# A decoder layer on one NeuronCore: the up-projection's seven products chained in one PSUM bank and interleaved across neighbouring gates, GpSimd's sums moved to VectorE, the down-projection's loads in a fixed order

## The chip, the cores and the metric

The kernel runs on one core of one Trainium2 chip. The metric is the device time of one execution in microseconds (us), lower is better. The time of a kernel is the median of its runs.

## What is computed

One hybrid decoder layer on 1024 tokens of width 1024, all in float32: two groups of token mixers (causal "forgetting" attention and a gated linear recurrence), one output projection, a residual with LayerNorm, a gated MLP with a causal convolution of width 3, and a last residual with LayerNorm. The change touches what follows the mixers:

```python
    mix = jnp.concatenate([o_a, o_r], axis=-1).astype(dtype) @ w_o[l]
    x = _layer_norm(DEEPNORM_ALPHA * x + mix, ln_mix_g[l], ln_mix_b[l])

    h = _causal_depthwise_conv(x @ w_up[l], conv_w[l], conv_b[l])
    a, u = jnp.split(h, 2, axis=-1)
    ffn = (jax.nn.gelu(a, approximate=False) * u) @ w_down[l]
    x = _layer_norm(DEEPNORM_ALPHA * x + ffn, ln_ffn_g[l], ln_ffn_b[l])
```

The width of the MLP is 2816, which is 22 tiles of 128 columns.

## The kernel before

Every float32 matrix product is made of three matmuls in a reduced format: both operands are split into a high and a low part (ScalarE rounds the high part, VectorE subtracts it to get the low part), and high·high, high·low and low·high are added up in PSUM. Tiles with a name ending in h and l, or the two halves of a tile `w` or `dw`, are such parts. A scheduler orders the instructions on each engine when the kernel is built; an engine executes its own list strictly in that order. `tc.issue_after` pins an instruction behind another one on the same engine. In the code `tt` and `stt` are VectorE's tensor_tensor and scalar_tensor_tensor, `gt_` is GpSimd's tensor_tensor, `act` and `nc.scalar.copy` are ScalarE, `mm` is TensorE.

**Output projection and first LayerNorm (L1156 to L1205).** The tokens stand in eight tiles of 128 rows. Tiles 4 to 7 are projected earlier, among the mixers; the loop at L1184 makes tiles 3, 2, 1, 0: 48 matmuls each (L1197), the residual on VectorE (L1199), LayerNorm (L267). `second_half`, `first_half` and `both_halves` then form the seven left operands that Strassen's scheme in Winograd's form needs for the MLP: "22", "s1", "11", "12", "s2", "s4", "s3". They are halves of token tiles or sums and differences of those halves. `unit` (L1145) transposes each with four TensorE transposes (L1149), and ScalarE and VectorE split the result (L1152, L1153).

**Up-projection (L1214 to L1342).** For each of 22 MLP tiles, called gates, `prep` (L1228) loads two weight tiles of 512 KB and forms four sums of weight halves on GpSimd (L1238 to L1241). `product` (L1245) splits one weight combination (L1248 on ScalarE, L1249 on VectorE) into one of eight buffers `w`, and issues 4 x 3 = 12 matmuls of 512 columns (L1254). A gate has seven products, in the order 1, 6, 2, 5, 7, 3, 4, into four PSUM banks `b[0]` to `b[3]`; odd and even gates use two sets of banks (`ps` and `pb` in the rows). Product 2 adds onto product 1 in `b[0]`, so ScalarE must first copy product 1 out (L1291, tile `s`); likewise product 3 follows a copy of product 5 (L1293). VectorE forms the other sums (L1295 to L1306); the convolution is one ScalarE activation and VectorE multiply-adds for each half of 512 tokens (L1280 to L1284); then GELU (L1310), the product of the two branches on GpSimd (L1311), every second gate four more sums on GpSimd (L1321 to L1324), and stores to `hd` in DRAM from GpSimd's queue.

**Down-projection (L1347 to L1524).** Seven products again, each of six chunks (`part`, L1426): a weight chunk `k0` or `k1` (`load_k`, L1376) and a stored chunk `ar` (`araw`, L1364) are loaded on SyncE's queue, both are split (L1372, L1373) into a ring of buffers `dw`, and up to 24 matmuls follow (L1446). Sums of weight halves are formed on GpSimd (L1433 to L1437, L1466). The residual rows `acc` are loaded back (L1452) and added. The last product (L1486) is followed tile by tile by the final LayerNorm (`finish`, L1398), whose last addition is GpSimd's (L1417).

## Time and profile before

| | |
|---|---|
| median of 3 runs | 1396.06 us (1393.99 to 1400.61) |
| the profiled execution, its own time | 1390.83 us |
| its span in the trace | 1389.0 us |
| mean granted TensorE clock | 0.975 of full speed |

The span is what the profiler's records cover; the 1.8 us between it and the execution's own time lie around it. Busy time of an engine is the time in which one of its instructions ran; a wait is the idle time just before an instruction, put down to the event that came last. TensorE's granted clock has two levels, 2.4 GHz (1.00 in the rows) and 1.2 GHz (0.50); a mean in between mixes the two. A VectorE or ScalarE instruction's record begins before the one ahead of it has ended, so the pace of a row of them is the distance of their starts and not the listed duration. PE is TensorE, DVE VectorE, ACT ScalarE, POOL GpSimd, SP SyncE.

### The profile page before, as it was taken

What the parts mean: (1) busy time and instruction counts of PE and PEld (TensorE: products, weight loads), DVE (VectorE), ACT (ScalarE), POOL (GpSimd) and SP (SyncE); (2) the same over time, 40 slices, a digit from 0 to 9 for tenths busy, and PEclk for the clock granted to TensorE, in tenths of its full rate; (3) what the DMA queues carried; (4) which work ended last, traced back from release to release, by engine and by line L of the source; (5) the groups of instructions that cost most, each with busy time, mean ns of one, the idle gap of its engine ahead of it and who ended that gap; (6) DMA issues with size and microseconds to landing.
All of it is one profiled execution on the core that took longest, in us unless ns stands there. A gap on an engine that the chain in (4) does not pass through costs nothing.

```text
span 1389.0 us, 17673 instructions
## 1 busy us (share of the span) xinstructions
PE 1298.2 (93%) x6457; PEld 1070.8 (77%) x6457; DVE 1080.2 (78%) x1517; ACT 632.4 (46%) x1045; POOL 528.9 (38%) x460
## 2 busy tenths in 40 slices
PE   6899999999999997999499999999999999899996
PEld 5888877877878886888487787778878787688886
DVE  8758686786646667668979999999999977665695
ACT  4246655654555645432353444444444443334351
POOL 4122222131332223003536556656655644850016
PEclk9999999999999999999799999999999999999998
DMA  8311211143433357423122223223223249633333
GB/s 291 137 31 31 76 31 61 41 123 127 97 101 95 83 126 207 155 84 118 76 91 92 82 92 114 99 91 114 80 76 111 99 127 390 252 97 96 99 99 114
DMA packets 68567, 156.45 MB, mean 113 GB/s; under 512 B 6720, under 2 KB 22080, under 8 KB 68480
## 3 DMA queue, kind: packets, MB, share of 16 engines
q1 hardware_dynamic: 57584, 116.78, 27.7%
q0 software_dynamic: 10896, 38.54, 7.4%
q8 instruction: 51, 0.84, 0.3%
q14 instruction: 36, 0.29, 0.1%
HBM read 99.98 MB, written 41.68 MB: 102 GB/s over the span
## 4 chain that ended last, share of the span: by engine, by line
PE 51%; DVE 25%; issue 8%; DMA 6%; ACT 6%; POOL 2%; SPq 1%; POOLq 0%; DVEq 0%; ACTq 0%
PE ps L1254 8%; PE pb L1254 7%; PE ps L235 5%; PE pb L1446 4%; PE ps L1446 4%; DVE w L1249 3%; PE pb L219 3%; PE ps L840 3%; PE pb L1197 2%; DVE yu L1282 2%; PE ps L961 2%; DMA ar<-hd 2%; DVE ya L1282 2%; PE pb L235 2%; PE pb L381 2%
## 5 line engine op out<-in xcount | busy, mean ns | idle before, releaser
L1249 DVE TENSOR_TENSOR w<-wt,w 128x512 fp32r<-128x512 f32 x88 | 128.1, 1455 | 5.8 <-ACT w L1248 5.7
L1249 DVE TENSOR_TENSOR w<-wraw,w 128x512 fp32r<-128x512 f32 x66 | 103.4, 1567 | 11.7 <-ACT w L1248 11.7
L209 POOL TENSOR_TENSOR wlo<-wraw,whi 128x1024 fp32r<-128x1024 f32 x20 | 51.9, 2593 | 135.2 <-ACT whi L208 107.5
L1446 PE MATMUL pb<-dw 128*128 128x512 f32 x396 | 94.3, 399 | 4.1 <-DVE dw L1373 4.1
L1446 PE MATMUL ps<-dw 128*128 128x512 f32 x396 | 92.9, 394 | 3.4 <-ACT dw L1372 2.0
L1446 PEld LDWEIGHTS pb<-dw 128*128 128x128 f32 x396 | 75.4, 191 | 22.6 <-DVE dw L1373 5.0
L1446 PEld LDWEIGHTS ps<-dw 128*128 128x128 f32 x396 | 74.1, 188 | 21.4 <-ACT dw L1372 2.4
L1311 POOL TENSOR_TENSOR ya<-ya,yu 128x1024 f32<-128x1024 f32 x21 | 50.8, 2420 | 101.8 <-ACT ya L1310 101.8
L1373 DVE TENSOR_TENSOR dw<-k,dw 128x1024 fp32r<-128x1024 f32 (+1 forms) x36 | 51.1, 1418 | 49.5 <-PE pb L1446 21.2
L1372 ACT CAST dw<-k 128x1024 fp32r<-128x1024 f32 (+1 forms) x36 | 35.0, 978 | 82.7 <-issue 33.5
L235 PE MATMUL ps<-xhi,whi 128*128 128x512 f32 x144 | 60.3, 419 | 1.3 <-DVE mo L739 1.3
L912 DVE TENSOR_REDUCE sml<-pb 128x1 f32<-128x896 f32 (+3 forms) x64 | 47.6, 751 | 15.7 <-PE pb L909 15.4
L1248 ACT CAST w<-wraw 128x512 fp32r<-128x512 f32 x66 | 40.6, 615 | 38.8 <-PE pb L1254 18.6
L235 PE MATMUL ps<-xlo,whi 128*128 128x512 f32 x144 | 58.0, 403 | 0.0
L219 PE MATMUL pb<-xhi,whi 128*128 128x512 f32 x176 | 57.7, 406 | 0.0
L219 PE MATMUL pb<-xhi,wlo 128*128 128x512 f32 x176 | 57.4, 400 | 0.0
L235 PE MATMUL ps<-xhi,wlo 128*128 128x512 f32 x144 | 57.4, 399 | 0.0
L1240 POOL TENSOR_TENSOR wt<-wraw,wt 128x512 f32<-128x512 f32 x22 | 29.3, 1330 | 72.3 <-DVE w L1249 72.1
L1248 ACT CAST w<-wt 128x512 fp32r<-128x512 f32 x88 | 54.3, 617 | 4.2 <-POOL wt L1238 1.7
L219 PE MATMUL pb<-xlo,whi 128*128 128x512 f32 x176 | 55.8, 398 | 0.0
L1373 DVE TENSOR_TENSOR dw<-ar,dw 128x1024 fp32r<-128x1024 f32 (+1 forms) x36 | 45.5, 1263 | 8.9 <-ACT dw L1372 8.6
L1372 ACT CAST dw<-ar 128x1024 fp32r<-128x1024 f32 (+1 forms) x36 | 35.1, 975 | 25.2 <-PE pb L1446 12.0
(439 smaller groups left out, 4082.1 us busy)
## 6 DMA issues: line engine op xcount, KB each, us to landing
wraw<-in_wup_dram SPq DMA_DIRECT2D x44, 512.0 KB, 3.6
ar<-hd SPq DMA_DIRECT2D x35, 512.0 KB, 3.6
wraw<-in_wt_dram SPq DMA_DIRECT2D x24, 512.0 KB, 3.7
hd<-sab POOLq DMA_DIRECT2D x22, 512.0 KB, 3.2
k<-in_wdn_dram SPq DMA_DIRECT2D x20, 512.0 KB, 10.1
hd<-ya POOLq DMA_DIRECT2D x11, 512.0 KB, 4.0
xres<-xin POOLq DMA_DIRECT2D x8, 512.0 KB, 4.1
wraw<-in_wo_dram SPq DMA_DIRECT2D x8, 512.0 KB, 5.3
```

The lines of the kernel that those rows point to most:

```text
L209: (nc.gpsimd.tensor_tensor if nlw[0] in PW else tt)(lo[:, ks], raw[:, ks], f(hi[:, ks]), ALU.subtract)
L219: mm(ps[:, h * 512:(h + 1) * 512], lhsT=l[:, k, :], rhs=r[:, k, h * 512:(h + 1) * 512], start=k == 0 and n == 0, stop=k == KT - 1 and n == 2)
L235: last_mm[0] = mm(ps, lhsT=l[:, k, :], rhs=r[:, k, h * 512:(h + 1) * 512], start=k == 0 and n == 0, stop=k == KT - 1 and n == 2)
L912: nc.vector.tensor_reduce(sml[:, 0:1], ps[:, 0:n], AX.X, ALU.max, negate=True)
L1248: nc.scalar.copy(sl[:, 0], w[n])
L1249: tt(sl[:, 1], w[n], f(sl[:, 0]), ALU.subtract)
L1254: last_mm[0] = mm(ps, lhsT=sl[:, wq, k], rhs=xq[:, k], start=bool(first and k == 0 and q == 0), stop=k == KH - 1 and q == 2, skip_group_ch ...
L1282: stt(y[:, o + d:o + 512], src[:, 0:512 - d], cw(t, 2 - d), y[:, o + d:o + 512], ALU.mult, ALU.add)
L1311: (tt if tail else gt_)(ya[:, hs], ya[:, hs], yu[:, hs], ALU.mult)
L1372: nc.scalar.copy(hi, raw)
L1373: tt(lo, raw, f(hi), ALU.subtract)
L1446: last_mm[0] = mm(sets[bset][t], lhsT=l[:, z, t * P:(t + 1) * P], rhs=r[:, z], start=bool(first and m + z == 0 and l is ah and r is bh), s ...
```

## The change

Five things change; the mixers before them stay as they are.

1. GpSimd's sums go to VectorE: the four weight sums of `prep`, the product after GELU, the four sums of every second gate, the sums of halves of token tiles ahead of the up-projection, and the sums of weight halves in the down-projection. GpSimd keeps its DMA queue, the reciprocal square roots and the last addition of `finish`.
2. In a gate the products 1, 6, 5, 3 are chained in one bank (`u[:, 0]`), with a ScalarE copy after 1, 6 and 5; 7 and 4 share another (`a[:, 1]`). VectorE's sums per gate fall from five to three, and the convolution runs over 1024 tokens at once. The order on TensorE is 6, 7, 5 of this gate, 1 of the next, 3 of this, 2 of the next, 4 of this.
3. The first gate is special: its weights are prepared before the output projection's loop, and its products 5 and 4, which need only the token tiles 4 to 7, run among the transposes of tiles 3, 2 and 1.
4. The LayerNorms of tiles 3, 2 and 1 become two VectorE instructions each; the statistics of tiles 2 and 1 are made on ScalarE, which writes its unused output over the projection's PSUM tile. Tile 0 is handled in column halves.
5. In the down-projection all loads are issued in program order (`fetch`), and the first residual is added after the second product's third chunk instead of before it.

```diff
-                gt_(y[:, R], y[:, L], y[:, R], ALU.add)
+                tt(y[:, R], y[:, L], y[:, R], ALU.add)
...
+            def sums(i):
 
                 y, z = xrs[i], xrs[4 + i]
                 tt(z[:, R], z[:, R], y[:, L], ALU.subtract)
-                gt_(z[:, L], y[:, L], z[:, L], ALU.subtract)
-                tt(y[:, L], y[:, R], z[:, R], ALU.subtract)
-                unit("12", y[:, R], i)
-                unit("s2", z[:, R], i)
-                unit("s4", y[:, L], i)
-                unit("s3", z[:, L], i)
+                tt(z[:, L], y[:, L], z[:, L], ALU.subtract)
+                s4s[i] = f1a.tile([P, 512], F32, name="s4", tag="u2") if i == 0 else y[:, L]
+                tt(s4s[i], y[:, R], z[:, R], ALU.subtract)
...
-                        for h in range(2):
-                            hs = slice(h * 512, (h + 1) * 512)
-                            mm(ps[:, hs], lhsT=lhs(i, j, k), rhs=r[:, k, hs],
-                               start=ki == 0 and nn == 0, stop=ki == KT - 1 and nn == 2)
-                stt(xr, xr, ALPHA, ps, ALU.mult, ALU.add)
-                layer_norm(cp, xr, xr, *gb1, add=nc.gpsimd.tensor_tensor if i in LNXP else tt, mode=LNX[i])
-                second_half(i)
-                if i < 3:
-                    first_half(i + 1)
-            first_half(0)
+                        last_mm[0] = mm(ps[:, hs], lhsT=lhs(i, j, k), rhs=r[:, k, hs],
+                                        start=k == KORD[0] and nn == 0, stop=k == KORD[-1] and nn == 2)
+                if i:
+                    stt(xr, xr, ALPHA, ps, ALU.mult, ALU.add)
+                    if i == 3:
+                        layer_norm(cp, xr, xr, *gb1, mode="S")
+                if i in (1, 2):
+                    mv = cp.tile([P, 4], F32, name="lnmv", tag="lnmv", bufs=2)
+                    act(ps, xr, AF.Copy, scale=1.0 / D, accum_out=mv[:, 0:1])
+                    act(mv[:, 3:4], mv[:, 0:1], AF.Copy, scale=-1.0)
+                    act(ps, xr, AF.Square, bias=mv[:, 3:4], accum_out=mv[:, 1:2])
+                    ts(mv[:, 1:2], mv[:, 1:2], 1.0 / D, LN_EPS, ALU.mult, ALU.add)
+                    nc.gpsimd.tensor_tensor(mv[:, 2:3], mv[:, 1:2], mhalf, ALU.pow)
+                    stt(xr, xr, mv[:, 0:1], gb1[0], ALU.subtract, ALU.mult)
+                    stt(xr, xr, mv[:, 2:3], gb1[1], ALU.mult, ALU.add)
+                if i == 0:
+                    st = cp.tile([P, 12], F32, name="lnst", tag="lnst", bufs=2)
+                    mv = cp.tile([P, 4], F32, name="lnmv", tag="lnmv", bufs=2)
+                    for h, hs in enumerate((L, R)):
+                        stt(xr[:, hs], xr[:, hs], ALPHA, ps[:, hs], ALU.mult, ALU.add)
+                        nc.vector.bn_stats(st[:, 6 * h:6 * h + 6], xr[:, hs])
+                    nc.vector.bn_aggr(mv[:, 0:2], st)
+                    ln_rstd(mv, False)
+                    for hs in (L, R):
+                        stt(xr[:, hs], xr[:, hs], mv[:, 0:1], gb1[0][:, hs], ALU.subtract, ALU.mult)
+                    for hs in (L, R):
+                        stt(xr[:, hs], xr[:, hs], mv[:, 2:3], gb1[1][:, hs], ALU.mult, ALU.add)
+                nc.gpsimd.dma_start(a1d[i], xr)
+                if i > 1:
+                    second_half(2 * i - 3)
+                    second_half(2 * i - 4)
+                if i:
+                    unit("11", xr[:, L], i)
+                    sums(i)
...
-                gt_(t12[:, 0], b12, b11, ALU.subtract)
-                gt_(t12[:, 1], b22, t12[:, 0], ALU.subtract)
-                gt_(t34[:, 1], b21, t12[:, 1], ALU.subtract)
-                gt_(t34[:, 0], b22, b12, ALU.subtract)
...
-                order = ((4, 3, 1, 1), (5, 2, 1, 0), (1, 0, 1, 0), (2, 0, 0, 1), (6, 1, 1, 0), (3, 2, 0, 1), (7, 1, 0, 1)) \
-                    if p == 0 else \
-                    ((1, 0, 1, 0), (6, 1, 1, 0), (2, 0, 0, 1), (5, 2, 1, 0), (7, 1, 0, 1), (3, 2, 0, 1), (4, 3, 1, 1))
...
+                def step(self, n):
+
+                    a, u, s1, u2, u4 = self.a, self.u, self.s1, self.u2, self.u4
                     if n == 1:
-                        nc.scalar.copy(s1, b[0])
+                        self.mul(1, u[:, 0])
+                        nc.scalar.copy(s1, u[:, 0])
+                    if n == 2:
+                        self.mul(2, a[:, 0])
+                        tt(a[:, 0], a[:, 0], s1, ALU.add)
+                    if n == 6:
+                        self.mul(6, u[:, 0], False)
+                        nc.scalar.copy(u2, u[:, 0])
+                    if n == 7:
+                        self.mul(7, a[:, 1])
                     if n == 5:
-                        nc.scalar.copy(s5, b[2])
+                        self.mul(5, u[:, 0], False)
+                        nc.scalar.copy(u4, u[:, 0])
+                    if n == 3:
+                        self.mul(3, u[:, 0], False)
+                        tt(u[:, 1], a[:, 1], u4, ALU.add)
+                        self.outs()
+                        self.conv(1)
+                    if n == 4:
+                        self.mul(4, a[:, 1], False)
+                        tt(a[:, 1], a[:, 1], u2, ALU.add)
+                        self.conv(0)
+                        self.end()
...
+                def end(self):
+                    j, (ya, yu) = self.j, self.y
+                    act(ya, ya, AF.Gelu)
+                    tt(ya, ya, yu, ALU.mult)
+                    half = NFF // 2
+                    if j < half:
+                        ys[j] = ya
+                        nc.gpsimd.dma_start(hd_[0, j], ya[:, L])
+                        return
                     m = j - half
                     ye = ys.pop(m)
-                    et_ = tt if tail else gt_
+                    tail = self.p == NFF - 1
                     sa, sb = (pl.tile([P, 2, 512], F32, name="sab", tag=tg)
                               for pl, tg in (((qkp, "ql"), (cp, "crow")) if tail else ((gv, "g0"), (gv, "g1"))))
-                    et_(sb[:, 0], ye[:, L], ye[:, R], ALU.subtract)
-                    et_(sa[:, 0], ye[:, R], ya[:, R], ALU.add)
-                    et_(sa[:, 1], sa[:, 0], ye[:, L], ALU.subtract)
-                    et_(sb[:, 1], ya[:, L], sa[:, 1], ALU.subtract)
+                    tt(sb[:, 0], ye[:, L], ye[:, R], ALU.subtract)
+                    tt(sa[:, 0], ye[:, R], ya[:, R], ALU.add)
+                    tt(sa[:, 1], sa[:, 0], ye[:, L], ALU.subtract)
+                    tt(sb[:, 1], ya[:, L], sa[:, 1], ALU.subtract)
...
+            work = chain(g.first_parts(5), g.first_parts(4))
+            for _ in range(2):
+                next(work)
+            for i in (3, 2, 1):
+                for n, src in (("12", xrs[i][:, R]), ("s2", xrs[4 + i][:, R]), ("s4", s4s[i]), ("s3", xrs[4 + i][:, L])):
+                    placed(n, src, i)
+                    next(work, None)
...
+                g, nxt = nxt, (Gate(p + 1) if p + 1 < NFF else None)
+                for n, of in ((6, g), (7, g), (5, g), (1, nxt), (3, g), (2, nxt), (4, g)):
+                    if of is not None:
+                        of.step(n)
...
+            def fetch(dst, src):
+
+                with tc.issue_after(last_ld[0].ins) if last_ld[0] is not None else ExitStack():
+                    last_ld[0] = nc.sync.dma_start(dst, src)
+
+            def bsum(dst, a, b):
+
+                with tc.issue_after(last_lo[0].ins):
+                    tt(dst, a, b, ALU.subtract)
...
-                    gt_(k0[c][:, :, L], k0[c][:, :, R], k0[c][:, :, L], ALU.subtract)
+                    bsum(k0[c][:, :, L], k0[c][:, :, R], k0[c][:, :, L])
                 if n == 6:
-                    gt_(k0[c][:, :, L], k1[c][:, :, R], k0[c][:, :, L], ALU.subtract)
+                    bsum(k0[c][:, :, L], k1[c][:, :, R], k0[c][:, :, L])
                 if n == 7:
-                    gt_(k0[c][:, :, R], k1[c][:, :, R], k0[c][:, :, R], ALU.subtract)
+                    bsum(k0[c][:, :, R], k1[c][:, :, R], k0[c][:, :, R])
...
-                        gt_(k0[c][:, :, L], k1[c][:, :, L], k0[c][:, :, L], ALU.subtract)
+                        tt(k0[c][:, :, L], k1[c][:, :, L], k0[c][:, :, L], ALU.subtract)
...
+                    if n == 5 and c == 2:
+                        residual(range(4), L)
+                        for t in range(4):
+                            stt(acc[:, t, L], acc[:, t, L], ALPHA, sets[0][t], ALU.mult, ALU.add)
```

Where the instructions stand is read from the built order of each engine. On ScalarE, around the end of a gate's last product 4: `ya` from the last bank is the convolution of the old gate, the COPY is the one that a product of the next gate waits for. Before:

```order
L1280 ACTIVATE yu_7725<-ps2_7710,ppt_76 128x512
L1248 CAST w_8032<-wraw_8018 128x512
L1280 ACTIVATE ya_7724<-ps3_7711,ppt_76 128x512
L1291 COPY s15_7879<-pb0_7865 128x512
L1248 CAST w_8048<-wt_8022 128x512
L1310 ACTIVATE ya_7724<-ya_7724 128x1024
```

and now:

```order
L1188 CAST w_7236<-wt_7082 128x512
L1316 ACTIVATE ya_7035<-ca_6808,ppt_76 128x1024
L1335 COPY u2_6955<-cu_6953 128x512
L1188 CAST w_7252<-wt_7083 128x512
L1188 CAST w_7267<-wt_7082 128x512
L1387 ACTIVATE ya_7035<-ya_7035 128x1024
```

The copy still stands right behind the old gate's convolution; it is now product 6's, which product 5 waits for, where it was product 1's, which product 2 waited for.

On GpSimd, at the end of the output projection (`wt` are weight sums, `xr` token tiles, `lnmv` the LayerNorm's small tiles). Before:

```order
L1238 TENSOR_TENSOR wt_6215<-wraw_6212,wraw_6211 128x512
L1239 TENSOR_TENSOR wt_6215<-wraw_6212,wt_6215 128x512
L1166 TENSOR_TENSOR xr_5063<-xr_5063 128x512
L1164 DMA a1d_61<-xr_5215 128x1024
L249 TENSOR_SCALAR lnmv_5881<-lnmv_5881 128x1
L250 TENSOR_TENSOR lnmv_5690<-lnmv_5690,half_80 128x1
```

and now:

```order
L1200 DMA a1d_61<-xr_5215 128x1024
L251 TENSOR_TENSOR lnmv_5690<-lnmv_5690,half_80 128x1
L251 TENSOR_TENSOR lnmv_5897<-lnmv_5897,half_80 128x1
L1255 DMA a1d_61<-xr_5836 128x1024
L1200 DMA a1d_61<-xr_5342 128x1024
```

The wide sums are gone from GpSimd there; what is left are stores and one-column roots.

On VectorE, at the change from the up-projection to the down-projection (L1348 is the last gate's sum after product 4, `dw` are the low parts of the first chunks):

```order
L1318 SCALAR_TENSOR_TENSOR yu_9382<-cu_9193,ppt_76,yu_9382 128x1022
L1348 TENSOR_TENSOR ca_9192<-ca_9192,u2_9195 128x512
L1492 TENSOR_TENSOR dw_9461<-k0_9431,dw_9460 128x1024
L1492 TENSOR_TENSOR dw_9457<-ar_9454,dw_9456 128x1024
L1318 SCALAR_TENSOR_TENSOR ya_9381<-ca_9192,ppt_76,ya_9381 128x1023
```

The first two low parts now stand behind a sum that waits for the last product of the up-projection.

## Rows read from the trace of the kernel before

**Rows 1.** The page's part 1: busy us, share of the span, instructions of each engine.

```profile
PE 1298.2 (93%) x6457; PEld 1070.8 (77%) x6457; DVE 1080.2 (78%) x1517; ACT 632.4 (46%) x1045; POOL 528.9 (38%) x460
```

**Rows 2.** Windows: stretch, its us, busy us of PE, PEld, DVE, ACT, POOL; clock; DMA.

```profile
653.40:695.50 42.10, 24.63 (x117) 19.96 (x116) 41.60 (x44) 15.01 (x24) 24.64 (x21) 0.74 0.16 63
695.50:720.90 25.40, 25.09 (x123) 20.62 (x122) 18.58 (x27) 13.11 (x24) 7.12 (x5) 0.95 0.30 89
720.90:1151.10 430.20, 416.94 (x1765) 334.74 (x1763) 403.10 (x506) 188.53 (x295) 237.47 (x181) 0.98 0.30 102
1151.10:1205.00 53.90, 46.35 (x189) 36.16 (x189) 36.66 (x32) 17.58 (x19) 40.18 (x18) 0.97 0.94 348
1205.00:1371.10 166.10, 166.10 (x736) 136.00 (x736) 118.49 (x136) 66.76 (x82) 48.24 (x34) 1.00 0.33 105
1371.10:1389.00 17.90, 6.93 (x34) 6.68 (x33) 6.50 (x14) 1.46 (x3) 5.73 (x7) 0.67 0.25 88
```

**Rows 3.** Waits, 720 to 1152 us: who waited for whom, total us, times, longest us.

```profile
PE ps L1254 <- ACT s L1291: 11.6, 7, 2.5
PE pb L1254 <- ACT s L1291: 1.5, 1, 1.5
...
ACT yu L1280 <- DVE pb L1300: 59.8, 11, 7.5
...
ACT ya L1280 <- DVE pb L1306: 14.8, 9, 1.6
```

**Rows 4.** Chain of waits, one gate of 84 matmuls: start, us, what.

```profile
1112.14 19.53 PE pb L1254 x84
```

**Rows 5.** Single lines: durations in ns, min/median/max; first and last start; forms.

```profile
L1249 DVE TENSOR_TENSOR w<-wt,w x88: 671/684/5977, 641.1 to 1130.2; 128x512 fp32r<-128x512 f32 x88
L1249 DVE TENSOR_TENSOR w<-wraw,w x66: 674/1406/3436, 639.1 to 1126.8; 128x512 fp32r<-128x512 f32 x66
...
L1153 DVE TENSOR_TENSOR xs1l<-ps,xs1h x4: 675/678/681, 650.2 to 686.4; 128x512 fp32r<-128x512 f32 x4
...
L1282 DVE SCALAR_TENSOR_TENSOR ya<-pb,ppt,ya x44: 729/735/740, 713.6 to 1137.8; 128x511 f32<-128x511 f32 x22, 128x510 f32<-128x510 f32 x22
...
L1280 ACT ACTIVATE ya<-pb,ppt x22: 772/777/782, 712.0 to 1135.5; 128x512 f32<-128x512 f32 x22
...
L1291 ACT COPY s<-pb x11: 571/576/587, 706.0 to 1115.0; 128x512 f32<-128x512 f32 x11
```

**Rows 6.** Timeline of DVE, 658 to 690 us: start, us, instruction, count, idle before.

```profile
658.72 3.34 DVE L276 TENSOR_TENSOR xr<-xr,b1r 128x1024 f32<-128x1024 f32 x1
...
667.15 4.53 DVE L272 SCALAR_TENSOR_TENSOR xr<-xr,lnmv,b1r 128x1024 f32<-128x1024 f32 x1
...
672.73 3.44 DVE L1249 TENSOR_TENSOR w<-wraw,w 128x512 fp32r<-128x512 f32 x1
...
687.03 1.22 DVE L276 TENSOR_TENSOR xr<-xr,b1r 128x1024 f32<-128x1024 f32 x1
688.17 0.68 DVE L1153 TENSOR_TENSOR x12l<-ps,x12h 128x512 fp32r<-128x512 f32 x1
688.77 0.68 DVE L1153 TENSOR_TENSOR xs4l<-ps,xs4h 128x512 fp32r<-128x512 f32 x1
689.37 4.10 DVE L1176 TENSOR_TENSOR xr<-xr 128x512 f32<-128x512 f32 x1
```

**Rows 7.** Timeline of PE, start of the down-projection: idle before it and releaser in brackets.

```profile
1154.92 28.58 PE L1446 MATMUL pb<-dw 128*128 128x512 f32 x116 [2.58 <-DVE dw L1373]
...
1190.96 2.13 PE L1446 MATMUL ps<-dw 128*128 128x512 f32 x8 [1.99 <-ACT dw L1372]
1194.22 4.00 PE L1446 MATMUL ps<-dw 128*128 128x512 f32 x16 [1.13 <-DVE dw L1373]
...
1201.59 1.20 PE L1446 MATMUL pb<-dw 128*128 128x512 f32 x4 [1.52 <-DVE dw L1373]
```

**Rows 8.** Timeline of PE, the last matmuls.

```profile
1374.36 6.88 PE L1486 MATMUL pb<-b,a 128*128 128x256 f32 x33 [3.22 <-DVE acc L1488]
```

More of the change, by code (lines that the diff above doesn't have):

```diff
@@ L1205, in body @@
+                nc.gpsimd.dma_start(a1d[i], xr)
[5 more added lines that the diff above has]
+                    sums(i)
             xp_es.close()
             big_es.close()
-            other = pool(top, "other", 1, space=PSUM)
-            def banks(q):
-                return [(small, other)[q].tile([P, 512], F32, name=f"p{'sb'[q]}{n}", tag=f"ps{n}") for n in range(4)]
+            up_es = ExitStack()
@@ L1244, in body, with product @@
             XOF = {1: "11", 2: "12", 3: "s4", 4: "22", 5: "s1", 6: "s2", 7: "s3"}
-            def product(w, n, ps, first, last):
-                sl = slot()
-                nc.scalar.copy(sl[:, 0], w[n])
-                tt(sl[:, 1], w[n], f(sl[:, 0]), ALU.subtract)
+            def product(sl, n, ps, first):
                 xh, xl = X[XOF[n]]
-                with tc.issue_after(last_mm[0].ins):
-                  for k in range(KH):
-                    for q, (wq, xq) in enumerate(((0, xh), (0, xl), (1, xh))):
-                      last_mm[0] = mm(ps, lhsT=sl[:, wq, k], rhs=xq[:, k], start=bool(first and k == 0 and q == 0),
-                           stop=k == KH - 1 and q == 2, skip_group_check=True)
+                for k in range(KH):
+                    with tc.issue_after(last_mm[0].ins):
+                        for q, (wq, xq) in enumerate(((0, xh), (0, xl), (1, xh))):
+                            last_mm[0] = mm(ps, lhsT=sl[:, wq, k], rhs=xq[:, k], start=bool(first and k == 0 and q == 0),
+                                            stop=k == KH - 1 and q == 2, skip_group_check=True)
+                    yield
@@ L1312, in gate @@
-                half = NFF // 2
-                if j < half:
-                    nc.gpsimd.dma_start(hd_[0, j], ya[:, L])
-                else:
+                        yield from self.parts(7, u[:, 1], False)
+                        tt(s1, u[:, 1], s1, ALU.add)
+                        tt(u[:, 1], s5, s1, ALU.add)
+                        tt(a[:, 1], a[:, 1], s1, ALU.add)
+                        self.outs()
+                        self.conv(1)
+                        self.conv(0)
+                        self.end()
@@ L1316, in gate, with first_step @@
+                def first_step(self, n):
+                    for _ in self.first_parts(n):
+                        pass
+                def end(self):
[7 more added lines that the diff above has]
+                        return
                     m = j - half
@@ L1330, in rest, with placed @@
-            def rest():
-                for i in (3, 2, 1, 0):
-                    both_halves(i)
-            gate(0, jorder[0], rest)
+            g = Gate(0)
+            def placed(n, src, i):
+                with tc.issue_after(last_mm[0].ins):
+                    unit(n, src, i)
+            work = chain(g.first_parts(5), g.first_parts(4))
[5 more added lines that the diff above has]
+                    next(work, None)
@@ new lines, in body @@
+            for _ in work:
+                pass
+            placed("11", xrs[0][:, L], 0)
+            sums(0)
+            placed("s2", xrs[4][:, R], 0)
+            work = g.first_parts(1)
+            for n, src in (("12", xrs[0][:, R]), ("s4", s4s[0]), ("s3", xrs[4][:, L])):
+                next(work)
+                placed(n, src, 0)
+            for _ in work:
+                pass
+        small_es.close()
+        ups.append(pool(up_es, "up1", 1, "right", space=PSUM))
+        for n in (6, 2, 3):
+            g.first_step(n)
@@ L1378, in load_k @@
                 src = wdn[q * NM + m:q * NM + m + n].rearrange("m p c -> p m c")
[L1379 removed]
+                fetch((k0, k1)[q][c][:, :, hs], src[:, :, hs])
+            dn = [pool(es, f"dn{q}", 1, ("left", "right")[q], space=PSUM) for q in range(2)]
             sets = [None, None]
             def fresh(q):
[L1384 removed]
+                sets[q] = [dn[q].tile([P, 512], F32, name=f"p{'sb'[q]}{n}", tag=f"ps{n}") for n in range(4)]
             fresh(0)
[L1387 removed]
             seq = [(1, 0, (0, L), 0, 1, 0), (5, 3, (0, L), 1, 1, 1), (6, 4, (0, L), 0, 0, 0), (2, 1, (1, L), 1, 1, 1),
```

164 lines of the change are left out of this document (89 added, 75 removed).

## The prediction

> **What bounds the kernel now.** I read the page's busy shares first, then busy time by stretch, then who waited for whom, and last the durations of single lines. The page says that TensorE is busy 93% of the span and VectorE 78% [rows 1], which hides that they take turns. By stretch [rows 2]: ahead of the first product of the up-projection (653.4 to 695.5 us) VectorE is busy 41.60 of 42.10 us and TensorE 24.63, at a mean clock of 0.74. In the first gate (695.5 to 720.9) TensorE is busy 25.09 of 25.40. In the other 21 gates (720.9 to 1151.1) both are nearly full: TensorE 416.94 and VectorE 403.10 of 430.20. At the start of the down-projection TensorE is idle 7.5 of 53.9 us; from 1205 to 1371 it never is. The last 17.9 us are the final LayerNorm.
>
> In the 21 gates the limit is TensorE at 19.53 us a gate [rows 4]. The gates take 430.2 / 21 = 20.49. All of TensorE's idle time there is eight waits, 13.1 us together, for one ScalarE copy, L1291 [rows 3]. That copy takes 0.58 us [rows 5]; it comes late because ScalarE, in strict order, stands before it waiting for VectorE sums of the old gate: 59.8 us on L1300, 14.8 us on L1306 [rows 3]. VectorE is late because some of its instructions are long. A low part (L1249, two SBUF operands) has a minimum of 0.67 us and takes up to 5.98; a low part of the same shape with one operand in PSUM (L1153) stays between 0.675 and 0.681 [rows 5]. GpSimd is busy 237 of these 430 us [rows 2]. I take the long ones as VectorE held up by GpSimd's reads.
>
> **The change part by part.** Paces: 512 columns follow each other at 0.60 us on VectorE, 1024 columns at 1.14 [rows 6]; a matmul of 512 columns at 19.53 / 84 = 0.2325 us [rows 4].
>
> *Up-projection, 21 gates.* VectorE's list per gate becomes 7 low parts, 4 weight sums, 3 sums and on average 2 of the sums for `hd`, 16 x 0.60 = 9.6 us, the GELU product 1.14, and four convolution passes of 1023 columns. This shape is not in the trace. The 511-column pass takes 0.735 us [rows 5], so twice that, 1.47, is the upper bound, and 0.735 itself the lower; I take 1.2, since the 1024-column sum of [rows 6] is the nearest. That is 4.8, and 15.5 us in all (bounds 13.7 and 16.6) against 19.53 of TensorE: VectorE is covered. GpSimd's wide work is gone, so nothing should stretch these.
>
> The copies grow from two to three a gate. Tightest is product 6's: it stands behind the old gate's convolution on ScalarE, as before, and product 5 waits for it. From the end of product 4, products 6 and 7 give 24 x 0.2325 = 5.58 us. In that time come a VectorE sum (0.60), the 1024-column convolution pass and the copy (0.58). The pass is 0.777 at 512 columns [rows 5], so between 0.78 and 1.55; taking 1.2, the sum is 2.4 and VectorE may be 3.2 us late. A late copy costs TensorE up to 2.5 us at a time [rows 3], and queued behind it on ScalarE are high parts of weights, which run several buffers ahead. A new wait, product 4 for VectorE's sum over `a[:, 1]`, has product 2 of the next gate, 2.79 us, between. So the pace should fall to 19.53, worth 430.2 - 21 x 19.53 = 20.1 us: 13.1 of waits, and 6.8 because 416.94 busy us hold only 410.1 us of matmuls, the rest going to a mean clock of 0.98 after the gaps [rows 2]. I leave 2 us for copies still late: 18. Bounds 0 (the pace stays) and 20.1.
>
> *Ahead of the up-projection.* Four instructions of [rows 6] lasted 3.34, 4.53, 3.44 and 4.10 us where their shapes take 1.22, 1.22, 0.68 and 0.68: 11.6 lost. VectorE takes over eight sums of token halves and the four weight sums of the second gate, 12 x 0.60 = 7.2, and two normalising passes, 2.3 (the first gate's weight sums come earlier, while TensorE is still projecting), and gives up four statistics of 512 columns, 2.4. Net 4.5 us shorter. Products 5 and 4 of the first gate, 24 x 0.2325 = 5.6 us, leave the TensorE-bound stretch for the VectorE-bound one; because the low parts behind must follow, I count 4.5 of it. Together 9; bounds 0 (VectorE's list no shorter, the products displaced) and 10.1. ScalarE's statistics hold a PSUM tile that tile 0's matmuls need; tile 0 is not used until VectorE has done the others, which hides some us of delay, and without that cover it costs what TensorE slips.
>
> *Start of the down-projection.* Four gaps of 2.58, 1.99, 1.13 and 1.52 us [rows 7] are 7.2, in a stretch where DMA is 0.94 busy [rows 2]. In order, each chunk of up to 1 MB comes in its turn, spaced by 5.58 us of matmuls, 188 GB/s against the 348 reached there. But VectorE now has a sum that waits for the last product ahead of the first two low parts: 0.60 + 2 x 1.14 = 2.9 us stay. Gain 4.3; bounds 0 and 7.2. SyncE's loads now wait for each other's buffers; behind a blocked one stand only later chunks.
>
> *Down-projection and end.* Twenty sums of 1024 and four of 512 columns come to VectorE, 20 x 1.14 + 4 x 0.60 = 25 us over 220 us in which it has 65 to spare; TensorE is full there and covers them. Per chunk VectorE needs 3 x 1.14 = 3.4 of 5.58 us; without the cover a sum costs 1.14. The final LayerNorm, with its 3.22 us gap [rows 8] behind GpSimd's additions, is left alone: 0.
>
> Sum: 18 + 9 + 4.3 = 31.3 us. The profiled execution took 1390.83 us (1389.0 of span and 1.8 around it) and becomes 1359.5. The median of the runs is 5.2 us above it, so I predict **1365 us**.
>
> **The rivals.** *The handoff stays* (no better pace). The copy still sits behind VectorE's last sum of the old gate, with the same two products of cover. For it: that distance is unchanged, and three copies can be late. Against it: VectorE's 15.5 of 19.53 us leave room, and nothing of 5.98 us stands in its list any more. Price 18 us: 1383.
>
> *VectorE becomes the bound*, slower. If the long low parts have another cause than GpSimd, VectorE keeps its 403.1 / 21 = 19.2 us a gate, adds 4.7 (four weight sums, the GELU product, two sums) and saves 1.9 (two sums fewer, four passes for eight): 22.0 a gate, decisive above 19.53. That is 462 instead of 430.2, +32; the stretch ahead then loses 2.6 (9 less 11.6), and 4.3 is gained: 1426. Against it stands the pair of lines in [rows 5]. The Trainium skill speaks for it: Perfetto Trace Analysis, Optimizing Scalar/DVE Operations, says that when VectorE is saturated, moving work to ScalarE or even GpSimd may make sense; this change does the reverse, and by that rule the time would be this rival's. The trace agrees that VectorE was saturated (94%), but a good part of that share is long instructions.
>
> *Loads in order stall.* If SyncE's queue is blocked by chunk buffers that come free late, TensorE waits for chunks in each of the first products. Taking the worst gap of [rows 7], 2.58 us, at ten of the twelve chunks of the first two products, that is 26 us, which eats most of the 31.3: 1391, no change.
>
> That the sums did not move is excluded: GpSimd's list has none of the wide ones left there.
>
> **How the numbers follow.** Forecast 0.70; handoff 0.13; VectorE the bound 0.06; loads stall 0.06; more than the sum of the upper bounds, for reasons I don't see, 0.05. Upper bounds together, 37.4 us, and runs 2 us under the median give 1357; I set the low end at 1355. The high end takes in the handoff case and 2 us: 1385. A measurement of this kernel tells about 0.5%, 7 us, from no change. Faster by more: 0.70 + 0.13 + 0.05 = 0.88. Same: 0.06. Slower: 0.06.
>
> **What would show it.** Right: TensorE's waits for ScalarE copies nearly gone in the up-projection; a gate at 19.5 to 19.7 us with the clock at 1.00; low parts with two SBUF operands all near 0.68 us; VectorE about 80% busy there; the first product, now among the transposes, some 15 us earlier, and the second gate some 9; one gap of about 3 us at the start of the down-projection; the end as before. Wrong: low parts still above 1 us, a gate above 20.2 us, or TensorE waiting on loads after the first chunk.

## The result and the profile after

| | before | changed |
|---|---|---|
| median of 4 runs, us | 1396.34 | 1362.57 |
| all runs, us | 1393.99 to 1400.61 | 1355.43 to 1364.11 |
| ratio, 95% interval | | 0.9745, 0.9703 to 0.9787 |
| profiled execution / its span, us | 1390.83 / 1389.0 | 1364.11 / 1362.3 |

The forecast was 1365 us, and the kernel became 2.55% faster. The two profiled executions differ by only 26.7 us, because they don't start alike. The mixers' instructions stand in the same order in both kernels on every engine up to there, and still one form of their products starts for the last time (the second time in each row) 8.5 us later in the changed kernel's profile. Before, then changed:

```profile
L907 PE MATMUL pb<-k,ea x48: 276/364/404, 355.5 to 604.2; 128*128 128x512 f32 x24, 128*128 128x256 f32 x16, 128*128 128x384 f32 x8
```

```profile
L908 PE MATMUL pb<-k,ea x48: 276/362/403, 361.9 to 612.7; 128*128 128x512 f32 x24, 128*128 128x256 f32 x16, 128*128 128x384 f32 x8
```

Over the 14 profiles of this study that mark lies anywhere from 604.2 to 612.7 us. So the stages are counted from it: **A** from that mark to the end of the up-projection, **B** from there to the end of the span. In the kernel before A is 546.9 us and B 237.9; in the changed one 519.5 and 230.1: 35.2 us gained behind the mixers.

The stretches of the changed kernel, columns as in [rows 2]:

```profile
680.70:722.20 41.50, 34.30 (x170) 26.75 (x169) 32.66 (x55) 18.76 (x34) 1.48 (x2) 0.92 0.28 89
722.20:1132.20 410.00, 408.46 (x1765) 330.64 (x1763) 335.34 (x434) 191.21 (x269) 27.75 (x41) 1.00 0.30 102
1132.20:1186.00 53.80, 51.72 (x218) 42.06 (x219) 40.10 (x41) 23.93 (x25) 2.15 (x3) 0.97 0.82 278
1186.00:1346.00 160.00, 159.64 (x708) 130.25 (x706) 124.78 (x148) 65.73 (x81) 23.58 (x24) 1.00 0.43 139
1346.00:1362.30 16.30, 5.70 (x33) 5.49 (x33) 6.50 (x14) 1.32 (x2) 5.52 (x7) 0.82 0.27 96
```

The second row holds the same 1765 matmuls as the third of [rows 2] and takes 410.0 us instead of 430.2, at a clock of 1.00. VectorE is busy 335 us instead of 403 although work was added to it. TensorE's waits in these gates, all of them, both in the last gate (before: [rows 3]):

```profile
PE ca L1281 <- DVE cu L1343: 0.9, 1, 0.9
PE cu L1281 <- ACT sv L1340: 0.7, 1, 0.7
```

The low parts of the weights, minimum/median/maximum in ns, answer to [rows 5]:

```profile
L1189 DVE TENSOR_TENSOR w<-wt,w x88: 672/681/693, 652.7 to 1108.7; 128x512 fp32r<-128x512 f32 x88
L1189 DVE TENSOR_TENSOR w<-wraw,w x66: 678/691/694, 682.7 to 1106.5; 128x512 fp32r<-128x512 f32 x66
```

No low part lasts longer than 0.694 us; the longest was 5.98. In the down-projection two gaps are left in place of the four of [rows 7], and the wait of [rows 8] is as it was (TensorE's timeline):

```profile
1134.28 29.45 PE L1565 MATMUL ps<-dw 128*128 128x512 f32 x120 [2.08 <-ACT dw L1491]
...
1203.54 24.31 PE L1565 MATMUL ps<-dw 128*128 128x512 f32 x104 [0.18 <-DVE dw L1492]
...
1349.05 5.70 PE L1604 MATMUL ps<-b,a 128*128 128x256 f32 x33 [3.23 <-DVE acc L1606]
```

### The profile page after: what moved, and what is told of

The parts are those of the page before. It is cut to its first block, busy times and chain, and to the rows that moved or that the text cites. A ratio compares the mean times of both kernels' runs of the same rounds, so it can differ in the third digit from the quotient of the medians.

```text
span 1362.3 us, 17337 instructions
## 1 busy us (share of the span) xinstructions
PE 1294.9 (95%) x6457; PEld 1070.0 (79%) x6457; DVE 1012.8 (74%) x1479; ACT 639.4 (47%) x1027; POOL 227.1 (17%) x274
## 4 chain that ended last, share of the span: by engine, by line
PE 74%; DVE 13%; DMA 4%; ACT 4%; POOL 2%; issue 2%; SPq 0%; POOLq 0%; DVEq 0%; ACTq 0%
PE cu L1281 18%; PE ca L1281 13%; PE ps L1565 6%; PE ps L236 6%; PE pb L1565 5%; PE pb L220 3%; PE ps L841 3%; PE pb L1228 3%; PE ps L962 2%; PE ps L662 2%; PE pb L236 2%; PE pb L382 2%; PE pb L908 2%; PE ps L944 2%; DVE e L621 2%
## 5 line engine op out<-in xcount | busy, mean ns | idle before, releaser
L1318 DVE SCALAR_TENSOR_TENSOR yu<-cu,ppt,yu 128x1023 f32<-128x1023 f32 (+1 forms) x44 | 56.2, 1276 | 14.9 <-ACT yu L1316 14.8
L1189 DVE TENSOR_TENSOR w<-wt,w 128x512 fp32r<-128x512 f32 x88 | 60.1, 683 | 9.2 <-ACT w L1188 9.1
L1492 DVE TENSOR_TENSOR dw<-k,dw 128x1024 fp32r<-128x1024 f32 (+1 forms) x36 | 40.7, 1131 | 35.2 <-PE pb L1565 21.6
L1281 PE MATMUL cu<-xs1h,w 128*128 128x512 f32 x176 | 60.1, 401 | 1.1 <-ACT xs1h L1153 1.1
L1318 DVE SCALAR_TENSOR_TENSOR ya<-ca,ppt,ya 128x1023 f32<-128x1023 f32 (+1 forms) x44 | 56.3, 1280 | 6.2 <-ACT ya L1316 5.0
L1491 ACT CAST dw<-ar 128x1024 fp32r<-128x1024 f32 (+1 forms) x36 | 35.2, 977 | 53.7 <-PE pb L1565 23.0
L1281 PE MATMUL ca<-x22h,w 128*128 128x512 f32 x176 | 58.9, 395 | 0.9 <-DVE cu L1343 0.9
L1281 PE MATMUL ca<-x12h,w 128*128 128x512 f32 x176 | 58.8, 395 | 0.8 <-DVE w L1189 0.8
L1281 PE MATMUL cu<-xs4h,w 128*128 128x512 f32 x176 | 58.8, 395 | 0.7 <-ACT sv L1340 0.7
L1281 PE MATMUL cu<-xs2h,w 128*128 128x512 f32 x176 | 58.8, 395 | 0.0
```

The lines of the kernel that those rows point to most:

```text
L1189: tt(sl[:, 1], w[n], f(sl[:, 0]), ALU.subtract)
L1281: last_mm[0] = mm(ps, lhsT=sl[:, wq, k], rhs=xq[:, k], start=bool(first and k == 0 and q == 0), stop=k == KH - 1 and q == 2, skip_group_ch ...
L1318: stt(y[:, d:], c[:, 0:S - d], cw(2 - d), y[:, d:], ALU.mult, ALU.add)
L1492: last_lo[0] = tt(lo, raw, f(hi), ALU.subtract)
```

## The experiments

Every run with its median, and A and B of its profile in us. The kernel before took 1392.7 to 1396.0 us (medians) beside them. Runs with the same instructions in a stage show what a single profile is good for: A is 519.2 to 521.0 in the changed kernel, E4, E5, E6 and E8 (E4 adds only GpSimd's memsets, E8 differs at the end of the last gate), B 228.5 in E7 and E9 and 230.1 to 230.2 in the changed kernel, E2, E3, E4, E10 and E12. B's two values are TensorE's clock. Behind the same wait of 2.08 us the same 120 matmuls take 29.45 us in the changed kernel (row above) and 27.89 in E7; the mean granted clock over the first 54 us of B is 0.97 and 1.00:

```profile
1126.96 27.89 PE L1562 MATMUL ps<-dw 128*128 128x512 f32 x120 [2.08 <-ACT dw L1488]
```

| | edit | median | A | B |
|---|---|---|---|---|
| before | | 1396.3 | 546.9 | 237.9 |
| changed | | 1362.6 | 519.5 | 230.1 |
| E1 | before, up-projection's sums on VectorE | 1372.2 | 523.0 | 239.1 |
| E2 | changed, those sums on GpSimd | 1359.2 | 519.0 | 230.1 |
| E3 | changed, idle GpSimd sums | 1410.2 | 568.4 | 230.2 |
| E4 | changed, idle GpSimd memsets | 1362.2 | 521.0 | 230.1 |
| E5 | changed, loads not in order | 1366.9 | 519.2 | 236.0 |
| E6 | changed, halves' sums on GpSimd | 1366.0 | 519.4 | 234.1 |
| E7 | changed, first gate unpinned | 1357.6 | 515.6 | 228.5 |
| E8 | changed, end and first chunk | 1356.4 | 519.4 | 224.2 |
| E9 | changed, not interleaved | 1405.6 | 562.4 | 228.5 |
| E10 | E2, not interleaved | 1406.0 | 565.6 | 230.1 |
| E11 | E7 and E8 together | 1350.2 | 515.7 | 224.2 |
| E12 | changed, statistics on VectorE | 1363.6 | 521.7 | 230.1 |

### E1 and E2: contention or chaining?

E1 is the kernel before with

```diff
-                gt_(t12[:, 0], b12, b11, ALU.subtract)
+                tt(t12[:, 0], b12, b11, ALU.subtract)
...
-                    (tt if tail else gt_)(ya[:, hs], ya[:, hs], yu[:, hs], ALU.mult)
+                    tt(ya[:, hs], ya[:, hs], yu[:, hs], ALU.mult)
...
-                    et_ = tt if tail else gt_
+                    et_ = tt
```

and the same for the other weight sums.

> The kernel before, its products, banks and order as they were; only GpSimd's weight sums, the product after GELU and the sums for hd in the up-projection go to VectorE (10 and a half wide instructions a gate). Theory (contention): GpSimd's reads stretch VectorE's instructions with two SBUF operands, so low parts of 1.4 us and more go to 0.68 us, VectorE's 17.5 us a gate fit, and the 21 gates fall from 20.49 us each to 19.6 to 19.9: 1378 to 1384 us. Rival (the chaining did it): VectorE gets 4.7 us a gate more to do and the copies come as late as before or later: 20.5 us a gate or more, 1396 us or above.

Measured: ratio to before 0.9828 (0.9807 to 0.9848), A shorter by 23.9 us. With the old order, the old banks and two copies a gate, TensorE no longer waits at all in the gates (406 us of the up-projection):

```profile
722.00:1128.00 406.00, 406.00 (x1757) 329.47 (x1756) 374.88 (x644) 190.93 (x292) 27.77 (x41) 1.00 0.31 105
```

TensorE is busy 406.00 of 406.00 us while VectorE is at 92%. The 21 gates take 408.1 us, 19.43 each. VectorE took over 4.7 us of work a gate, and its busy time per gate still fell, from 403.1 / 21 = 19.2 us to 374.88 x 19.43 / 406 = 17.9. The low parts that had a median of 1406 ns and a maximum of 3436 ([rows 5]) are short; the one that is not stands at 676 us, ahead of the gates:

```profile
L1249 DVE TENSOR_TENSOR w<-wraw,w x66: 680/685/3440, 642.5 to 1105.6; 128x512 fp32r<-128x512 f32 x66
```

The theory holds, and its range was too cautious: the moved sums alone bring the gates to TensorE's pace.

E2 is the changed kernel with

```diff
+            et_ = tt if early else gt_
-            tt(t12[:, 0], b12, b11, ALU.subtract)
+            et_(t12[:, 0], b12, b11, ALU.subtract)
...
-                    tt(ya, ya, yu, ALU.mult)
+                    et_(ya, ya, yu, ALU.mult)
```

and the same for the other weight sums and the sums for `hd`.

> The changed kernel with the weight sums of gates 1 to 21, the product after GELU and the sums for hd back on GpSimd; chaining and interleaving stay. Theory (contention): low parts are long again (some above 1.4 us), copies come late, the gates take 20.0 to 20.5 us: 1373 to 1384 us. Rival (chaining and interleaving gave the slack): low parts may be long, but VectorE has 4.7 us a gate less to do, and the gates stay at 19.5 to 19.6 us: 1360 to 1366 us.

Measured: 1359.17 us, ratio 0.9736 (0.9722 to 0.9751), A 519.0: nothing lost. But the low parts are long again:

```profile
L1190 DVE TENSOR_TENSOR w<-wt,w x88: 673/692/2144, 648.7 to 1104.3; 128x512 fp32r<-128x512 f32 x88
L1190 DVE TENSOR_TENSOR w<-wraw,w x66: 682/1258/2611, 678.6 to 1102.0; 128x512 fp32r<-128x512 f32 x66
```

```profile
717.70:1127.70 410.00, 408.46 (x1765) 330.73 (x1763) 301.09 (x293) 191.74 (x269) 247.57 (x182) 1.00 0.30 102
```

The rival holds here. GpSimd is busy 248 us (237 before), VectorE only 301, and the same 410.0 us come out. Either half of the change is enough for the gates; the second one adds nothing there.

### E3 and E4: the contention by itself

To the changed kernel, behind each gate's stores on GpSimd's queue:

```diff
+                    with tc.issue_after(dm.ins):
+                        for _ in range(11):
+                            gt_(sc, f(X["22"][0][:, 0, 0:384]), f(X["s1"][0][:, 1, 0:384]), ALU.add)
```

In E4 the last line is `nc.gpsimd.memset(sc, 0.0)`. The other engines' instructions and their order stay the same.

> The changed kernel plus 11 sums a gate on GpSimd of two SBUF operands of 128 x 384, from tiles that nobody writes, into a tile that nobody reads: the contention alone, no handoff. Theory (contention): VectorE's instructions with two SBUF operands stretch from 0.68 to over 1 us on the mean while GpSimd works, those with a PSUM operand don't; with some 12 us of GpSimd a gate VectorE loses 4 to 6 us a gate, on 16 us, and the gates take 19.6 to 20.5 us: 1365 to 1384 us. Rival (only the handoffs to and from GpSimd cost): nothing stretches, 1360 to 1366 us.

> As the run with idle sums, but the 11 instructions a gate are memsets of 128 x 384 that read nothing. Theory (GpSimd's reads of SBUF are what hold VectorE up): nothing stretches, low parts at 0.68 us, 1360 to 1366 us. Rival (any wide GpSimd instruction does): low parts above 0.8 us on the mean.

Measured: E3 1410.23 us, slower than before (ratio 1.0106, 1.0079 to 1.0133); E4 1362.17 us. VectorE's lines in 375 us of E3's gates (columns: busy us, mean ns, idle before), and GpSimd's:

```profile
L1189 DVE TENSOR_TENSOR w<-wt,w 128x512 fp32r<-128x512 f32 x70 | 68.0, 980 | 0.0
L1189 DVE TENSOR_TENSOR w<-wraw,w 128x512 fp32r<-128x512 f32 x51 | 62.7, 1229 | 8.3 <-ACT w L1188 8.1
L1181 DVE TENSOR_TENSOR wt<-wraw 128x512 f32<-128x512 f32 x18 | 23.9, 1326 | 0.0
...
L1332 DVE TENSOR_TENSOR ca<-ca,sv 128x512 f32<-128x512 f32 x18 | 12.5, 694 | 2.3 <-PE ca L1281 2.3
L1179 DVE TENSOR_TENSOR wt<-wraw 128x512 f32<-128x512 f32 x18 | 12.4, 691 | 0.6
```

```profile
L1391 POOL TENSOR_TENSOR scr<-x22h,xs1h 128x384 f32<-128x384 f32 x176 | 213.6, 1214 | 12.9
```

The first three lines, with two SBUF operands, rise to 0.98 to 1.33 us on the mean; L1332, of the same shape with one operand in PSUM, stays at 0.694, although GpSimd's sums run during 85% of its time. L1179 has two SBUF operands and stays short: in this trace it never runs beside one of these sums. No data passes between GpSimd's sums and the other engines. In E4 nothing stretches:

```profile
L1189 DVE TENSOR_TENSOR w<-wraw,w x66: 681/691/694, 677.8 to 1102.2; 128x512 fp32r<-128x512 f32 x66
```

A is 48.9 us longer in E3, and the 21 gates (20 of them with idle sums) take 457.2 us, 21.8 each, beyond the theory's range. VectorE is busy 416.90 of these 457.2 us, and TensorE waits again (715 to 1140 us), most of all for L1335, the copy of product 6:

```profile
PE cu L1281 <- ACT u L1335: 16.6, 8, 2.2
PE ca L1281 <- DVE cu L1343: 9.5, 9, 1.5
```

The contention is shown, and so is that writing alone does not bring it about: memsets of the same width, 0.42 us each where a sum takes 1.21, stretch nothing.

### E9 and E10: what the interleaving does

```diff
-                for n, of in ((6, g), (7, g), (5, g), (1, nxt), (3, g), (2, nxt), (4, g)):
+                for n, of in ((6, g), (7, g), (5, g), (3, g), (4, g), (1, nxt), (2, nxt)):
```

E10 makes the same edit in E2.

> The changed kernel with TensorE's order 6, 7, 5, 3, 4 of this gate and then 1, 2 of the next: chained in the same banks, not interleaved; all sums on VectorE. Theory (the interleaving covers the copies): product 3 stands right behind product 5 and waits in every gate for product 5's copy, 0.58 us and its start, 0.7 to 1.2 us a gate; the gates take 20.2 to 20.8 us, the time is 1376 to 1390 us. Rival (with GpSimd quiet, VectorE and ScalarE are early enough in any order): 19.5 to 19.7 us a gate, 1360 to 1366 us.

> As the run without interleaving, and the up-projection's sums are on GpSimd again, so that only the chaining and the wider convolution remain of the up-projection's change. Theory (the interleaving is what makes GpSimd's contention harmless): VectorE's long low parts come on top of the wait for product 5's copy, the gates take 0.3 us or more longer than without interleaving and with the sums on VectorE: 6 us or more above that run. Rival (VectorE's shorter list is what makes it harmless): the same time as that run within 3 us.

Measured: 1405.56 and 1405.97 us, 0.9% slower than before (ratios 1.0090, 1.0060 to 1.0121, and 1.0092, 1.0064 to 1.0119). TensorE's waits in E9's gates:

```profile
PE ca L1281 <- DVE cu L1343: 18.2, 21, 2.3
PE cu L1281 <- ACT sv L1340: 14.2, 21, 0.7
```

Two waits a gate, 0.68 us for the copy of product 5 and 0.87 us for VectorE's sum that needs this copy and stands ahead of product 4. A is 42.9 us longer, 2.0 us a gate. The waits are 32.4 us, 1.6 in the changed kernel; the rest is with the matmuls around a wait: the first behind it lasts 0.50 instead of 0.39 us, and the last ahead of it runs out its 0.39 us, where otherwise the next one starts 0.23 us after it. The theory named the first wait and missed the second. E10's time is E9's within their spread, against the theory; its 21 gates take 455.1 us, E9's 453.0, 0.1 us more a gate, although single low parts reach 4.7 us. So the chaining costs two waits a gate by itself, and the interleaving hides them. It is not the interleaving that makes GpSimd's contention harmless. That leaves VectorE's shorter list (busy 301 of 410 us in E2) or the chained products with their other banks and copies; no run separates these two.

### E5 and E6: the start of the down-projection

E5 takes the order out of `fetch`, E6 puts `bsum` and the last product's sums back on GpSimd:

```diff
-                with tc.issue_after(last_ld[0].ins) if last_ld[0] is not None else ExitStack():
-                    last_ld[0] = nc.sync.dma_start(dst, src)
+                nc.sync.dma_start(dst, src)
```

```diff
-                with tc.issue_after(last_lo[0].ins):
-                    tt(dst, a, b, ALU.subtract)
+                gt_(dst, a, b, ALU.subtract)
```

> The changed kernel with the down-projection's loads issued in the scheduler's order again, as before; the sums of weight halves stay on VectorE. Theory (the order of the loads took the gaps away): TensorE's gaps at the start of the down-projection are 5 us or more in all again instead of 2.3, and the time is 3 to 5 us above the changed kernel's. Rival (the gaps were VectorE's low parts, held up by GpSimd's sums): the gaps stay at 2 to 3 us and the time within 2 us.

> The changed kernel with the down-projection's sums of weight halves back on GpSimd; the loads stay in order. Theory (order of the loads): gaps of 2 to 3 us at the start of the down-projection, time within 2 us of the changed kernel. Rival (GpSimd's sums hold up the low parts): low parts of 1.14 us stretch to 2 us and more, the gaps are 5 us or more, 3 to 5 us slower.

Measured: 1366.86 us (ratio 0.9804, 0.9770 to 0.9837) and 1365.99 us (0.9806, 0.9767 to 0.9846); B is 5.9 and 4.0 us longer than in the changed kernel. E5's gaps, then E6's:

```profile
1132.90 1.19 PE L1564 MATMUL ps<-dw 128*128 128x512 f32 x4 [1.14 <-ACT dw L1490]
...
1170.01 4.00 PE L1564 MATMUL pb<-dw 128*128 128x512 f32 x16 [1.01 <-DVE dw L1491]
1175.88 3.06 PE L1564 MATMUL ps<-dw 128*128 128x512 f32 x12 [1.88 <-ACT dw L1490]
1180.35 19.65 PE L1564 MATMUL pb<-dw 128*128 128x512 f32 x84 [1.40 <-ACT dw L1490]
...
1207.71 4.68 PE L1564 MATMUL ps<-dw 128*128 128x512 f32 x19 [1.31 <-DVE dw L1491]
```

```profile
1129.54 29.46 PE L1564 MATMUL ps<-dw 128*128 128x512 f32 x120 [2.08 <-ACT dw L1490]
...
1201.12 4.14 PE L1564 MATMUL ps<-dw 128*128 128x512 f32 x10 [2.48 <-DVE dw L1491]
```

Both parts count. Without the order, gaps of 7 us are back, and ScalarE waits 14.3 us for loads of `ar` (1131 to 1212 us) where in the changed kernel's stretch it waits for none. The clock hides some of the loss: it is 1.00 in E5's first 54 us, so that beside E7 and E9 (228.5) its B is 7.5 us longer. With the order, GpSimd's sums stretch VectorE's low parts of 1024 columns, 1.22 us in the changed kernel, and one gap of 2.48 us comes up, behind which the granted clock is 0.88 (1201.1 to 1215.3 us; 1.00 in that stretch of the changed kernel). The low parts in 171 us of E6 from the start of the down-projection:

```profile
L1491 DVE TENSOR_TENSOR dw<-ar,dw 128x1024 fp32r<-128x1024 f32 x29 | 51.4, 1772 | 7.3 <-ACT dw L1490 7.3
```

Of E6's 4.0 us 2.3 are idle time, nearly all the rest lies around that gap. Its theory falls on this point; its rival had the size, though not gaps of 5 us.

### E7 and E12: ahead of the second gate

E7 takes the `next(work)` out of the loop over tiles 3, 2, 1, so that the products 5 and 4 of the first gate are no longer pinned among their transposes.

```diff
-            for _ in range(2):
-                next(work)
             for i in (3, 2, 1):
                 for n, src in (...):
                     placed(n, src, i)
-                    next(work, None)
```

> The changed kernel with products 5 and 4 of the first gate behind the transposes of tiles 3, 2 and 1 instead of among them; its weights are still prepared early. Theory: the 24 matmuls, 5.6 us, fill TensorE's waits for VectorE; without them the second gate starts 4 to 5 us later. Rival: VectorE's list ends at the same time and TensorE catches up, 0 to 1 us.

Measured: 1357.56 us (ratio 0.9736, 0.9707 to 0.9765), A shorter by 3.9 us: neither expectation. Nor did the edit do what its expectation says: without the pins the scheduler still ran both products among the transposes, in larger pieces: product 5 in 1 and 11 matmuls, product 4 in 6, 1 and 5, with 28 transposes between the first and the last of these 24 matmuls and 28 more ahead of product 1 (24 and 36 in the changed kernel). From the start of product 1 to the end of the up-projection the changed kernel takes 1132.2 - 702.47 = 429.7 us, E7 1124.9 - 698.72 = 426.2, so most of the gain (3.5 of 3.9 us) comes behind these products, where product 1 runs among tile 0's transposes. The changed kernel, then E7, from there on:

```profile
702.47:722.20 19.73, 17.53 (x73) 13.61 (x74) 11.45 (x18) 6.83 (x12) 0.00 (x0) 0.91 0.29 102
```

```profile
698.72:714.90 16.18, 15.64 (x73) 12.57 (x74) 11.13 (x18) 7.00 (x13) 0.00 (x0) 1.00 0.37 126
```

The same 73 matmuls take 3.55 us less: 1.66 of it idle time, the rest a clock that stays at 1.00 instead of 0.91. What it is worth to have these products in this stretch at all was not measured.

E12 gives the statistics of tiles 2 and 1 to VectorE:

```diff
-                if i in (1, 2):
-                    mv = cp.tile([P, 4], F32, name="lnmv", tag="lnmv", bufs=2)
...
                 if i:
                     stt(xr, xr, ALPHA, ps, ALU.mult, ALU.add)
-                    if i == 3:
-                        layer_norm(cp, xr, xr, *gb1, mode="S")
+                    layer_norm(cp, xr, xr, *gb1, mode="S")
```

> The changed kernel with the LayerNorm statistics of tiles 2 and 1 on VectorE (four statistics of 512 columns and two that combine them) instead of ScalarE. Theory (VectorE sets the end of this stretch): four times 0.60 us come back, the second gate starts 2 to 3 us later, from 519 us behind the last mixer product to the up-projection's end to 521 or 522. Rival (ScalarE's two passes over the tile, while the projection's bank is held, cost as much as they save): the stretch is the same within 1 us or shorter.

Measured: 1363.59 us; A 521.7, as the theory has it, but only 0.7 above E4, where all engines but GpSimd have the changed kernel's instructions. Not settled by one profile.

### E8 and E11: what is left

E8 makes `finish` add on VectorE, starts the ring of buffers `dw` with those that the last gate's last product does not hold, and splits the first chunk ahead of that gate's last sums:

```diff
-                    gt_(yf[:, hs], yf[:, hs], b2[:, hs], ALU.add)
+                    tt(yf[:, hs], yf[:, hs], b2[:, hs], ALU.add)
...
-            ring = [(f1a, f"w{n}") for n in range(3)] + [(f1a, "trw")] + ...
+            ring = [(f1a, "trw"), (wp, "wlo"), (wp, "wlo"), (f1a, "w0"), ...
...
+            load_k(0, 0, L)
+            ar0 = araw(0, 0, chunks[0][1])
+            head0 = dsplit2(ar0, rt(2), rt(2)) + dsplit2(k0[0][:, :, L], rt(2), rt(2))
+            with tc.issue_after(last_lo[0].ins):
+                g.conv(1)
+                g.done()
```

> The changed kernel with two more edits: the final LayerNorm's additions on VectorE instead of GpSimd, and the first chunk of the down-projection split ahead of the last gate's last sums, into buffers that the last product does not hold. Theory: TensorE's waits of 3.2 us near the end and of 2.1 us at the start of the down-projection go, 4 to 6 us faster than the changed kernel: 1356 to 1359 us. Rival: VectorE, 9.6 us more loaded in the last product, is late for its additions to acc, and the wait near the end stays at 2 to 3 us: 1360 to 1362 us.

Measured: 1356.35 us (ratio 0.9728, 0.9695 to 0.9761), B shorter by 5.9 us. Of the waits 0.11 us at the start, 0.26 right behind and 0.51 near the end are left:

```profile
1131.31 27.30 PE L1579 MATMUL ps<-dw 128*128 128x512 f32 x116 [0.26 <-DVE dw L1496]
...
1342.27 4.19 PE L1618 MATMUL ps<-b,a 128*128 128x256 f32 x33 [0.51 <-DVE acc L1620]
```

The last row is the one of 3.23 us and 5.70 us above: with the wait gone, the 33 matmuls behind it take 4.19 us.

> The changed kernel with the final LayerNorm's additions on VectorE, the first chunk of the down-projection split early, and the first gate's products 5 and 4 behind the transposes instead of among them. Theory (the two gains lie in different stages and add): 5.9 us at the start and end of the down-projection and 3.9 us ahead of the second gate, 1350 to 1354 us. Rival (they overlap or are spread of the mixers): 1355 us or more.

Measured, five runs: 1350.17 us (1346.83 to 1352.15), ratio 0.9689 (0.9665 to 0.9712). A is E7's and B is E8's: the gains add. This version beats both kernels.

## Why the prediction was right

**The 21 gates**, -18 predicted, 20.2 us gained: the upper bound, since the 2 us set aside for late copies were not needed. VectorE's 15.5 us a gate were 335.34 / 21 = 16.0. The reason was half right. That the long low parts were GpSimd's reads is shown by E1, E3 and E4. That the gates needed GpSimd's sums gone is not: E2 has the same pace with low parts up to 2.6 us. The step took the change's two halves as one; each is enough alone. Product 6's copy, named as the tightest, never made TensorE wait in these gates; where VectorE is held up in this order (E3), it is the one that TensorE waits for most, as the prediction had it. Without the interleaving (E9) both waits lie behind product 5, which the prediction did not look at.

**The stretch ahead**, -9 predicted, 720.9 - 604.2 = 116.7 us before and 722.2 - 612.7 = 109.5 after: 7.2 gained. Against the mark, the first product starts 20.8 us earlier (15 was forecast) and the second gate 7.2 (9). VectorE is busy 32.66 of 41.50 us (680.7 to 722.2) where it was 41.60 of 42.10, and from 640 us to the second gate none of its instructions lasts over 1.4 us. No run undoes the parts of this stretch one by one, so how the 7.2 us divide between VectorE's shorter list and the displaced products is not shown. The size held, though the order pinned by hand gave away 3.9 us of it (E7), which the term of 4.5 us for the displaced products did not foresee.

**The start of the down-projection**, -4.3 predicted; gaps fell by 7.5 - 2.26 = 5.2 us and B by 7.8. Two steps of it failed. The gap that stayed was forecast as VectorE's, 2.9 us behind the sum L1348; it was 2.08 us behind a ScalarE copy into a buffer that the last product still read, and E8, with other buffers and the chunk split earlier, removed it. ScalarE's row in the changed kernel:

```profile
1132.23 1.05 ACT L1491 CAST dw<-k 128x1024 fp32r<-128x1024 f32 x1 [1.86 <-PE ca L1281]
```

And the moved sums of halves were costed at nothing, as covered; E6 shows them to be worth 4.0 us, by low parts stretched as in the gates. Of the 7.8 us, 6.4 lie in the first 80 us of the down-projection, 5.2 of idle time and 1.2 with the matmuls around the gaps; 1.2 are the last 33 matmuls (6.88 and 5.70 us), at a clock of 0.67 and 0.82 in the last rows, which the prediction has no term for; 0.2 come after them.

**The end**, 0 predicted: 3.22 us before, 3.23 after, as said.

**The rivals.** The handoff did not stay. VectorE did not become the bound, but E3 comes near that rival: it was priced at 22.0 us a gate and 1426 us, and E3 has 457.2 / 21 = 21.8 and 1410, with VectorE busy 91% of the gates. The loads did not stall; order was worth 5.9 us (E5), 7.5 at the same clock. The prediction quoted the Trainium skill, Perfetto Trace Analysis, Optimizing Scalar/DVE Operations, against the change and left out how the passage goes on: since GpSimd and VectorE share an SBUF read port, moving work between the two might not help. E1 shows it in reverse, by 1.7%. The Trainium skill, SBUF — State Buffer, Who interferes with whom, states the rule that [rows 5] suggested: a VectorE instruction with two SBUF inputs contends with a GpSimd instruction that reads SBUF, not with one that only writes. E3 and E4 agree: 0.98 to 1.33 us against 0.694 at most.

**The total** came out 2.4 us from the forecast, in part by luck. Behind the mark 35.2 us were gained, 3.9 more than the sum of 31.3: 2.2 in the gates and 3.5 in the down-projection, where two steps failed, less 1.8 ahead of them. And the median, not the profile, was forecast: by its profile alone, with 8.5 us more in the mixers, the gain reads as 26.7 us. Why the mixers vary so much was not looked into.

## What to carry to other kernels

Before believing that an engine is full, compare its instructions of one shape with operands in PSUM and in SBUF: here some 19.2 - (17.9 - 4.7) = 6.0 of VectorE's 19.2 us a gate were waiting for GpSimd's reads, and handing it more work made it less busy. Two remedies for one wait don't add; undo each alone before crediting both. A chain in one bank saves sums but needs other work between its links: without it the same kernel lost 43 us, more than the whole change gains.
